# The second output projection: weights, row blocks and first splits in another order, and another place for every second row block's operands

## The chip, the cores and the metric

The kernel runs on one core of one Trainium2 chip. The metric is the time of one execution on the device in microseconds (us); three runs of a kernel are given by their median. Engine names are those of the profile: PE multiplies matrices, PEld loads its weights, DVE, ACT and POOL work elementwise, SP issues most of the transfers. A transfer is called a load when it goes from device memory (DRAM) to the chip's own memory.

## What is computed

Two layers of an encoder over 1024 rows of 1024 numbers. A layer is a token mixer, a layer norm, a gated feed-forward part and a second layer norm. The first mixer is latent attention, the second is differential attention: two softmax maps per head, subtracted. This is the end of the second mixer, where the change lies:

```python
o = jnp.einsum('bhqk,bkhe->bqhe', a.astype(v.dtype), v)   # a = p[:, 0] - lam * p[:, 1]
o = _rmsnorm(o, g_sub) * (1.0 - lambda_init)
return o.reshape(b, s, DIFF_HEADS * DIFF_V) @ w_o
...
h = _layernorm(ALPHA * h + mix, ln_mix_g[i], ln_mix_b[i])
```

All of it is float32. The kernel writes a float32 operand as a high part (cast to a shorter format) plus a low part (what the cast lost) and multiplies high by high, high by low and low by high, so that one product of 128 x 128 by 128 x 512 is three matmuls.

## The kernel before

**Stages.** Mixer A, its output projection (`out_proj`), feed-forward 0, mixer B, its output projection (class `OutProj`), feed-forward 1. Only `OutProj` and the place where it is called change.

**What surrounds the change.** Mixer B goes through 8 heads of 8 row blocks (128 rows each), the last head in the order `LAST_ORDER = (6, 7, 4, 5, 2, 3, 0, 1)`. For a row block and a head PE makes the scores (`s_b`, line 220), DVE adds the bias and takes the extreme (`mx_b`, line 223), ACT exponentiates (line 228), DVE takes reciprocals (line 1429), POOL scales one map (line 1430) and DVE subtracts it (line 1431); PE transposes the result (`pt_b`), ACT and DVE split it (`pth_b`, `ptl_b`, lines 251 and 252), and PE multiplies with the values (`o_b`, line 263) for two row blocks at once. The scores have three PSUM tiles. A table (`fill`, filled by `at`) hangs further work on the steps of this loop ("slots"); within that, a scheduler that simulates the engines sets the order in which each engine's queue is written. Each engine works through its queue in order.

**The output projection.** For each row block the output is a sum over heads of `o` times `w_o`. For the row blocks 6 and 7 (`first` and `second`) the first six heads (`HEADS = 6`) are summed in `early`, within the last head's loop, from a copy of `o` in DRAM (`of`); the last two heads follow in `late`, from the tile `bo` that is still on the chip. The other six row blocks are done whole in `rest`, which also makes the layer norm. A product is `zp_a` (line 418); `oh_a` and `ol_a` are the high and low part of `o`, made by ACT (line 406) and DVE (line 407) in `split`; `z_a` is the row block of x to which DVE adds the product (line 426).

**Where the tiles lie.** The weights of a head are a high and a low half of 0.5 MB each. Those of the heads 0 to 5 are one tile of 1 MB each (`wo`) in the projection's pool, whose space was that of the transposed x (`xT`) until the last values (`bv`) are made. Those of the heads 6 and 7 lie in a ring of three pairs of tiles (`who`, `wlo`) that also holds the operands of row block 6 and that mixer B's weights and the feed-forward part use before and after. The operands of row block 7 have a tile of the pool (tag `oh`), those of the blocks 4, 5, 2, 3, 0 and 1 a tile each of the five "big" tiles (1 MB each), which also hold the rows `z_a` of two blocks at a time and the norm's factors (`gb`, two loads issued by POOL, line 448).

**The start of a row block.** `of` issues the load of `o`, takes the tiles, issues the load of the rows x and makes the split at once, for the row blocks 6 and 7 in the constructor:

```python
for tb in LAST_ORDER[:2]:
    self.of(tb)
```

All loads named here but those of `gb` are issued by SP, into one queue.

Of the kernel before, what the change touches and what calls it, by code (L numbers as in the profile page):

```python
# [38 lines left out]
LAST_ORDER = (6, 7, 4, 5, 2, 3, 0, 1)  # L39
# [3 lines left out]
def trunk(  # L43
# [66 lines left out]
    def big_tile(name, dt=F32R):  # L110
        return big.tile([P, 2, 1024], dt, tag="big", name=name)
# [13 lines left out]
    def small(name, n=1):  # L125
        return sp.tile([P, 2], F32, tag="small", name=name, bufs=22)[:, :n]
# [159 lines left out]
    def out_proj(side, w_o, o_dram, x_src, x_dst, lng, lnb, xo):  # L286


        with tc.tile_pool(name="op0", bufs=2, side=side, reuse_waits="tile") as pool:
# [21 lines left out]
            for tb in LAST_ORDER:  # L311
                nm = f"a0_{tb}"
                of = pool.tile([P, H, P], F32, tag="of", name=f"of_{nm}", bufs=2)
                src = o_dram[tb // 2][:, :, (tb % 2) * P:(tb % 2) * P + P]
                nc.sync.dma_start(of, src.rearrange("h p q -> p h q"))
                ot = pool.tile([P, 2, D], F32R, tag="oh", name=f"oh_{nm}").rearrange("p a (h q) -> p a h q", h=H)
                oh, ol = ot[:, 0], ot[:, 1]
# [31 lines left out]
    class OutProj:  # L349
# [5 lines left out]
        def __init__(self, side, w_dr, o_dram, o_here, x_src, x_dst, scale):  # L355
            self.st = ExitStack()
            self.pool = self.st.enter_context(tc.tile_pool(name="op1", bufs=2, side=side, reuse_waits="tile"))
            self.o_dram, self.o_here, self.x_src, self.x_dst, self.scale = o_dram, o_here, x_src, x_dst, scale
            self.oh, self.z, self.sums, self.m = {}, {}, {}, {}
            for tb in LAST_ORDER[:2]:  # L360
                self.of(tb)
            self.wo = []
            for h in range(H):
                if h < self.HEADS:
                    t = self.pool.tile([P, 2, D], F32, tag=f"wo{h}", name=f"wo1_{h}", bufs=1)
                    nc.sync.dma_start(t, w_dr[h])
                    t = t.bitcast(F32R)
                    self.wo.append((t[:, 0], t[:, 1]))
                else:
                    t = [wp.tile([P, D], F32, tag=f"w{p}", name=f"w{p}o1_{h}") for p in "hl"]  # L370
                    for p in range(2):
                        nc.sync.dma_start(t[p], w_dr[h][:, p])
                    self.wo.append([x.bitcast(F32R) for x in t])

        def of(self, tb):

            nm, n = f"a1_{tb}", self.HEADS
            k = LAST_ORDER.index(tb)
            first = k < 2
            of = (wp if k < 4 else self.pool).tile(  # L380
                [P, H, P], F32, tag="wr" if k < 4 else f"z{LAST_ORDER[k % 2]}", name=f"of_{nm}", bufs=2 if k < 4 else 1,
            )[:, :n]
            src = self.o_dram[tb // 2][:n, :, (tb % 2) * P:(tb % 2) * P + P]
            nc.sync.dma_start(of, src.rearrange("h p q -> p h q"))
            if tb == LAST_ORDER[0]:
                hl = [wp.tile([P, D], F32R, tag=f"w{p}", name=f"o{p}_{nm}") for p in "hl"]
            else:
                if first:
                    t = self.pool.tile([P, 2, D], F32R, tag="oh", name=f"oh_{nm}", bufs=1)
                else:  # L390
                    t = big_tile(f"oh_{nm}")
                hl = [t[:, p] for p in range(2)]
            self.oh[tb] = [t.rearrange("p (h q) -> p h q", h=H) for t in hl]
            if first:
                self.z[tb] = self.pool.tile([P, D], F32, tag=f"z{tb}", name=f"z_{nm}", bufs=1)
            elif k % 2 == 0:
                self.pair = big_tile(f"z_{nm}", F32)
            if not first:
                self.z[tb] = self.pair[:, k % 2]
            nc.sync.dma_start(self.z[tb], self.x_src[tb * P:(tb + 1) * P, :])  # L400
            self.sums[tb] = small(f"sum_{nm}", 2)
            self.split(tb, slice(0, n), of)

        def split(self, tb, hs, o):
            oh, ol = (t[:, hs] for t in self.oh[tb])
# [655 lines left out]
    early = ast.enter_context(tc.tile_pool(name="a1e", bufs=1))  # L1061
# [130 lines left out]
    with ast as st:  # L1192
# [97 lines left out]
        def at(slot, fn, *args):  # L1290
            fill.setdefault(slot, []).append(lambda: fn(*args))
# [57 lines left out]
    with ExitStack() as st:  # L1349
# [165 lines left out]
        first, second = LAST_ORDER[:2]  # L1515
# [6 lines left out]
        b = 8 * (H - 1) - 2  # L1522
        at(b, begin_out)
        for slot, what, args in (
            (3, "early", (first, (0, 1))), (4, "early", (first, (2, 3))), (5, "early", (first, (4, 5))),
            (8, "early", (second, tuple(range(H - 2)))), (9, "late", (first,)),
        ):
            at(b + slot, lambda what, *a: getattr(proj[0], what)(*a), what, *args)
# [97 lines left out]
```

## Time and profile before

| | |
|---|---|
| median of three runs | 2262.74 us (2262.04 to 2263.79) |
| profiled execution, time | 2264.72 us |
| profiled execution, span of the core | 2263.0 us |
| mean granted clock of PE | 0.998 |
| PE busy | 2239.2 us, 99% of the span |
| PEld / DVE / ACT / POOL busy | 1912.2 / 1545.3 / 1014.7 / 776.2 us |
| matmuls | 11410 |
| chain that ended last, PE's share | 95% |
| q1, the queue that SP issues into | 277.44 MB, 34.6% of 16 engines |

The table is the page of the profiled execution, the only one of which there is a trace; its time lies 1.98 us above the median of the runs. Busy time counts from an instruction's start to its modelled end; PE's instructions overlap, so that a busy PE can still wait for operands. The part of the trace that matters here lies between 1480 and 1680 us: to about 1549 us the rest of mixer B runs together with `early` and the first `late`, from there to 1620 us `rest`, and behind it feed-forward 1.

### The profile page before, as it was taken

To read this page: it belongs to the slowest core of one execution; us is meant where nothing else is said; L and a number is where in the kernel's file an instruction comes from. 1 tells how busy PE (TensorE), PEld (TensorE's weight loads), DVE (VectorE), ACT (ScalarE), POOL (GpSimd) and SP (SyncE) were. 2 spreads that over 40 slices of the span, in tenths; PEclk is the share of its full clock that TensorE was granted. 3 is DMA by queue.
4 is the path that set the end of the run, shared out by engine and by line. 5 is a ranking of instruction groups with operands and counts; after the bars stand their busy time and mean duration, and the time that the engine had idled before them with its cause. 6 is when DMAs were issued, how large, how long until landed. Compare 5 with 4: busy or idle time off the path is not lost.

```text
span 2263.0 us, 31059 instructions
## 1 busy us (share of the span) xinstructions
PE 2239.2 (99%) x11410; PEld 1912.2 (84%) x11410; DVE 1545.3 (68%) x2894; ACT 1014.7 (45%) x2097; POOL 776.2 (34%) x626
## 2 busy tenths in 40 slices
PE   8999999999999999999999999999999999999998
PEld 8999998888888888888888898878788888888886
DVE  5676765596766667777576667576787656658778
ACT  4455664352333334444465656564432333334444
POOL 2232341114444440455432424221114444430561
PEclk9999999999999999999999999999999999999999
DMA  5010125434435338454320212063344232238443
GB/s 204 14 35 31 42 71 188 147 122 155 171 133 202 115 127 327 181 194 157 99 52 22 69 34 62 23 223 124 128 144 165 82 108 102 103 113 325 162 180 150
DMA packets 105545, 287.76 MB, mean 127 GB/s; under 512 B 7968, under 2 KB 30112, under 8 KB 94896
## 3 DMA queue, kind: packets, MB, share of 16 engines
q1 hardware_dynamic: 101552, 277.44, 34.6%
q0 software_dynamic: 3840, 8.33, 1.4%
q8 instruction: 90, 1.47, 0.3%
q14 instruction: 63, 0.52, 0.1%
HBM read 204.47 MB, written 77.07 MB: 124 GB/s over the span
## 4 chain that ended last, share of the span: by engine, by line
PE 95%; DVE 2%; DMA 1%; issue 1%; ACT 1%; POOL 0%; SPq 0%; DVEq 0%; POOLq 0%; ACTq 0%
PE gb L548 15%; PE ga L548 10%; PE gc L548 10%; PE dw L872 7%; PE dx L872 5%; PE s_a L220 4%; PE zp_a L418 3%; PE s_b L220 3%; PE dv L872 3%; PE dy L872 3%; PE bp L145 3%; PE bp L143 3%; PE bp L144 3%; PE o_a L263 2%; PE o_b L263 2%; PE hq L1123 2%
## 5 line engine op out<-in xcount | busy, mean ns | idle before, releaser
L504 ACT CAST op_g<-gr 128x512 fp32r<-128x512 f32 x240 | 146.9, 621 | 377.3 <-PE gb L548 189.9
L505 POOL TENSOR_TENSOR op_g<-gr,op_g 128x512 fp32r<-128x512 f32 x104 | 146.0, 1409 | 254.1 <-ACT op_g L504 143.9
L505 DVE TENSOR_TENSOR op_h<-rh,op_h 128x512 fp32r<-128x512 f32 x152 | 142.3, 962 | 50.0 <-ACT op_h L504 50.0
L548 PE MATMUL ga<-xh_m,op_g 128*128 128x512 f32 x512 | 168.2, 389 | 0.0
L872 PE MATMUL dw<-op_w_t,op_h 128*128 128x512 f32 x660 | 151.3, 390 | 0.0
L504 ACT CAST op_h<-rh 128x512 fp32r<-128x512 f32 x152 | 91.8, 619 | 124.6 <-PE dx L872 34.9
L872 PEld LDWEIGHTS dw<-op_w_t,op_h 128*128 128x128 f32 x660 | 123.6, 188 | 25.9 <-DVE op_h L505 0.3
L228 ACT ACTIVATE l_b<-l_b,mx_b 128x256 f32<-128x256 f32 (+7 forms) x128 | 99.4, 777 | 73.2 <-DVE mx_b L223 71.2
L505 POOL TENSOR_TENSOR op_w_b<-rw_b,op_w_b 128x512 fp32r<-128x512 f32 x44 | 64.5, 1488 | 175.1 <-ACT op_w_b L504 167.8
L505 DVE TENSOR_TENSOR op_g<-gr,op_g 128x512 fp32r<-128x512 f32 x136 | 112.0, 827 | 17.4 <-ACT op_g L504 17.2
L872 PE MATMUL dx<-op_w_b,op_h 128*128 128x512 f32 x528 | 121.5, 390 | 1.0 <-DVE op_w_b L505 1.0
L1430 POOL TENSOR_SCALAR l_b<-l_b,rb,cst 128x128 f32<-128x128 f32 (+3 forms) x64 | 52.8, 825 | 198.9 <-DVE rb L1429 187.5
L872 PEld LDWEIGHTS dx<-op_w_b,op_h 128*128 128x128 f32 x528 | 98.8, 188 | 23.0 <-DVE op_w_b L505 2.6
L548 PE MATMUL gb<-t3h_f,op_g 128*128 128x512 f32 x352 | 115.5, 389 | 1.0 <-DVE tmp L637 1.0
L548 PE MATMUL gb<-t2h_f,op_g 128*128 128x512 f32 x352 | 115.4, 390 | 0.4 <-DVE op_g L505 0.4
L548 PE MATMUL gc<-t1h_f,op_g 128*128 128x512 f32 x352 | 115.6, 389 | 0.1
L548 PE MATMUL gb<-t4h_f,op_g 128*128 128x512 f32 x352 | 115.5, 389 | 0.0
L548 PE MATMUL gc<-b22h_f,op_g 128*128 128x512 f32 x352 | 115.3, 389 | 0.0
L505 POOL TENSOR_TENSOR op_g<-s,op_g 128x512 fp32r<-128x512 f32 x40 | 56.1, 1403 | 166.4 <-ACT op_g L504 158.4
L548 PEld LDWEIGHTS ga<-xh_m,op_g 128*128 128x128 f32 x512 | 96.1, 188 | 20.0
L143 PE MATMUL bp<-xT_f,h_wb 128*128 128x512 f32 x256 | 101.8, 398 | 0.0
L144 PE MATMUL bp<-xT_f,h_wb 128*128 128x512 f32 x256 | 101.5, 397 | 0.0
(388 smaller groups left out, 6690.8 us busy)
## 6 DMA issues: line engine op xcount, KB each, us to landing
gr<-in_w_gu SPq DMA_DIRECT2D x44, 1024.0 KB, 6.8
rh<-h_dr SPq DMA_DIRECT2D x28, 1024.0 KB, 4.8
h_dr<-sh SPq DMA_DIRECT2D x22, 1024.0 KB, 5.1
h_dr<-hp SPq DMA_DIRECT2D x22, 768.0 KB, 4.1
tt<-in_w_dn SPq DMA_DIRECT2D x22, 512.0 KB, 7.5
rh<-h_dr SPq DMA_DIRECT2D x12, 768.0 KB, 4.3
wo_dr<-op_pwo SPq DMA_DIRECT2D x16, 512.0 KB, 3.4
z<-xs_dr SPq DMA_DIRECT2D x16, 512.0 KB, 12.0
```

The lines of the kernel that those rows point to most:

```text
L143: T.matmul(ps_out, lh, rh, start=(i == 0), stop=False)
L144: T.matmul(ps_out, lh, rl, start=False, stop=False)
L145: T.matmul(ps_out, ll, rh, start=False, stop=(i == n - 1))
L220: T.matmul(s[:, :w], lh, rh[:, ks], start=(j == 0), stop=(j == len(q_pass) - 1))
L228: ends["exp"] = A.activation(l[:, :n], l[:, :n], AF.Exp, bias=mx, scale=-1.0, accum_out=sm).ins
L263: T.matmul(po[:, c], a, b[:, j % 2, c], start=st, stop=sp_, skip_group_check=True)
L418: T.matmul(m, a[:, h, :], self.wo[h][w][:, c], start=(start and h == heads[0] and a is oh and w == 0), stop=(stop and h == heads[-1] and a ...
L504: turns["cast"] = A.copy(hi, src).ins
L505: return eng.tensor_tensor(lo, src, f32(hi), ALU.subtract).ins
L548: T.matmul(o, w[:, a, k * P:(k + 1) * P], x[b][:, k, :], start=(first and k == 0 and (a, b) == (0, 0)), stop=(k == 3 and a == 1), skip_gro ...
L872: T.matmul(o, h[:, a, c], w[:, b_], start=(first and (a, b_) == (0, 0)), stop=(last and a == 1), skip_group_check=True,).ins for a, b_ in ...
L1430: G.tensor_scalar(l1[:, :n], l1[:, :n], r[:, 1:2], nlam, ALU.mult, ALU.mult)
```

## The change

- The weights of the heads 0 and 1 now lie in the ring and those of the heads 2 to 7 in the pool's tiles.
- The constructor issues the loads in this order: row block 6's `o`, the weights of the heads 0 to 5, with row block 6's rows x ahead of head 6, row block 7's `o` and its rows, and the weights of the heads 6 and 7. The scheduler puts some of them elsewhere, as shown below.
- The splits of the row blocks 6 and 7 are no longer made in the constructor. They are called `first_split` and hang on the table 0 and 6 slots behind it.
- Two of the three parts of `early` for row block 6 hang one slot earlier (2 and 3 instead of 3 and 4).
- The row blocks 5, 3 and 1 have their operands in the pool's one tile `oh`, as row block 7 had; of the big tiles the blocks 4, 2 and 0 take one each.

```diff
-            for tb in LAST_ORDER[:2]:
-                self.of(tb)
+            self.of(LAST_ORDER[0])
             self.wo = []
             for h in range(H):
-                if h < self.HEADS:
+                if h == 6:
+                    self.load_z(LAST_ORDER[0])
+                if h == self.HEADS:
+                    self.of(LAST_ORDER[1])
+                    self.load_z(LAST_ORDER[1])
+                if h > 1:
                     t = self.pool.tile([P, 2, D], F32, tag=f"wo{h}", name=f"wo1_{h}", bufs=1)
...
-                if first:
+                if k % 2:
                     t = self.pool.tile([P, 2, D], F32R, tag="oh", name=f"oh_{nm}", bufs=1)
                 else:
                     t = big_tile(f"oh_{nm}")
...
+            self.sums[tb] = small(f"sum_{nm}", 2)
+            if first:
+                self.loaded[tb] = of
+            else:
+                self.load_z(tb)
+                self.split(tb, slice(0, n), of)
+
+        def load_z(self, tb):
             nc.sync.dma_start(self.z[tb], self.x_src[tb * P:(tb + 1) * P, :])
-            self.sums[tb] = small(f"sum_{nm}", 2)
-            self.split(tb, slice(0, n), of)
+
+        def first_split(self, tb):
+            self.split(tb, slice(0, self.HEADS), self.loaded.pop(tb))
...
-            (3, "early", (first, (0, 1))), (4, "early", (first, (2, 3))), (5, "early", (first, (4, 5))),
+            (0, "first_split", (first,)),
+            (2, "early", (first, (0, 1))), (3, "early", (first, (2, 3))), (5, "early", (first, (4, 5))),
+            (6, "first_split", (second,)),
             (8, "early", (second, tuple(range(H - 2)))), (9, "late", (first,)),
```

No instruction is added or removed. Up to the last head of mixer B and from feed-forward 1 on, every engine has the same instructions in the same order; between them three places matter.

**SP's queue, at the constructor, before** (the number behind a name is the head or the row block, the last one counts tiles; 128x1024 is 0.5 MB, 128x2048 is 1 MB):

```order
L372 DMA wlo_6_14976<-wo_dr_95 128x1024
L372 DMA who_6_14975<-wo_dr_95 128x1024
L384 DMA of_a_4_15581<-o_dr_2_87 128x6x128
L372 DMA wlo_7_14980<-wo_dr_96 128x1024
L400 DMA z_a_6_14950<-xs_dr_98 128x1024
L400 DMA z_a_7_14958<-xs_dr_98 128x1024
L366 DMA wo_0_14963<-wo_dr_89 128x2048
L366 DMA wo_1_14965<-wo_dr_90 128x2048
```

**The same place after:**

```order
L376 DMA who_0_14952<-wo_dr_89 128x1024
L376 DMA wlo_0_14953<-wo_dr_89 128x1024
L376 DMA wlo_1_14957<-wo_dr_90 128x1024
L376 DMA who_1_14956<-wo_dr_90 128x1024
L370 DMA wo_2_14960<-wo_dr_91 128x2048
L370 DMA wo_3_14962<-wo_dr_92 128x2048
L370 DMA wo_4_14964<-wo_dr_93 128x2048
L370 DMA wo_5_14966<-wo_dr_94 128x2048
L412 DMA z_a_6_14950<-xs_dr_98 128x1024
L412 DMA z_a_7_14972<-xs_dr_98 128x1024
L370 DMA wo_6_14975<-wo_dr_95 128x2048
L370 DMA wo_7_14977<-wo_dr_96 128x2048
```

Head 0's weights stand where head 6's stood, and ahead of head 2's stand 2 MB of loads, where ahead of head 0's there were 2.9 MB; row block 4's `o` and the rows x of blocks 6 and 7 have moved behind head 5's.

**PE's queue, the first products of the projection, before** (`zp_a_6_0` is the left half of row block 6's product, `zp_a_6_1` the right half):

```order
L263 MATMUL o_b_3_15030<-pth_b_6_3_14938,bvl_7_14865 128x128
L220 MATMUL s_b_4_0_0_15059<-bk_10192,bq_10190 128x320
L220 MATMUL s_b_4_0_0_15059<-bk_10192,ql_10195 128x320
L418 MATMUL zp_a_6_0_0_15160<-wo_0_14963,oh_a_6_14948 128x512 x2
L418 MATMUL zp_a_6_0_0_15160<-wo_0_14963,ol_a_6_14949 128x512
L418 MATMUL zp_a_6_1_0_15167<-wo_0_14963,oh_a_6_14948 128x512 x2
L418 MATMUL zp_a_6_1_0_15167<-wo_0_14963,ol_a_6_14949 128x512
L148 MATMUL pt_b_6_0_15085<-ident,l_b_6_0_14890 128x128 x4
```

**And after** (ahead of the first row shown stand the five products of head 0 that need its weights alone, and ahead of these the third of the last head's four scores of row block 6):

```order
L431 MATMUL zp_a_6_0_0_15108<-who_1_14956,oh_a_6_14948 128x512
L431 MATMUL zp_a_6_0_0_15108<-wlo_1_14957,oh_a_6_14948 128x512
L431 MATMUL zp_a_6_0_0_15108<-who_1_14956,ol_a_6_14949 128x512
L431 MATMUL zp_a_6_1_0_15115<-who_0_14952,ol_a_6_14949 128x512
L431 MATMUL zp_a_6_1_0_15115<-who_1_14956,oh_a_6_14948 128x512
L431 MATMUL zp_a_6_1_0_15115<-wlo_1_14957,oh_a_6_14948 128x512
L431 MATMUL zp_a_6_1_0_15115<-who_1_14956,ol_a_6_14949 128x512
L431 MATMUL zp_a_6_0_0_15108<-wo_2_14960,oh_a_6_14948 128x512 x2
L431 MATMUL zp_a_6_0_0_15108<-wo_2_14960,ol_a_6_14949 128x512
L431 MATMUL zp_a_6_1_0_15115<-wo_2_14960,oh_a_6_14948 128x512 x2
L431 MATMUL zp_a_6_1_0_15115<-wo_2_14960,ol_a_6_14949 128x512
L220 MATMUL s_b_6_1_1_14908<-bk_10192,bq_10190 128x448
```

Before, the first product stands behind all scores of the row blocks 6 and 7; now 18 products (heads 0 to 2) stand ahead of the fourth score of row block 6.

**PE's queue in `rest`, where row block 2 follows row block 5, before** (`xTp_a` are transposes of a finished row block):

```order
L418 MATMUL zp_a_5_1_0_15707<-who_7_14979,oh_a_5_15674 128x512
L148 MATMUL xTp_a_4_0_15746<-ident,z_a_4_15584 128x128 x4
L148 MATMUL xTp_a_4_1_15754<-ident,z_a_4_15584 128x128 x4
L418 MATMUL zp_a_2_0_0_15772<-wo_0_14963,oh_a_2_15764 128x512 x2
L418 MATMUL zp_a_2_1_0_15798<-wo_0_14963,oh_a_2_15764 128x512 x2
L418 MATMUL zp_a_2_0_0_15772<-wo_0_14963,oh_a_2_15764 128x512
```

**And after:**

```order
L431 MATMUL zp_a_5_1_0_15707<-wo_7_14977,oh_a_5_15674 128x512 x3
L431 MATMUL zp_a_2_0_0_15772<-who_0_14952,oh_a_2_15764 128x512
L431 MATMUL zp_a_2_0_0_15772<-wlo_0_14953,oh_a_2_15764 128x512
L431 MATMUL zp_a_2_0_0_15772<-who_0_14952,oh_a_2_15764 128x512
L431 MATMUL zp_a_2_0_0_15772<-who_1_14956,oh_a_2_15764 128x512
L431 MATMUL zp_a_2_0_0_15772<-wlo_1_14957,oh_a_2_15764 128x512
L431 MATMUL zp_a_2_0_0_15772<-who_1_14956,oh_a_2_15764 128x512
L431 MATMUL zp_a_2_0_0_15772<-wo_2_14960,oh_a_2_15764 128x512 x3
L431 MATMUL zp_a_2_0_0_15772<-wo_3_14962,oh_a_2_15764 128x512 x3
L148 MATMUL xTp_a_4_0_15746<-ident,z_a_4_15584 128x128 x4
```

The transposes of block 4 have moved from the boundary of two row blocks to the middle of the second one's first half, and the left half's products now stand together.

More of the change, by code (lines that the diff above doesn't have):

```diff
@@ L358, in __init__ @@
             self.o_dram, self.o_here, self.x_src, self.x_dst, self.scale = o_dram, o_here, x_src, x_dst, scale
-            self.oh, self.z, self.sums, self.m = {}, {}, {}, {}
-            for tb in LAST_ORDER[:2]:
-                self.of(tb)
+            self.oh, self.z, self.sums, self.m, self.loaded = {}, {}, {}, {}, {}
+            self.of(LAST_ORDER[0])
             self.wo = []
             for h in range(H):
-                if h < self.HEADS:
+                if h == 6:
[4 more added lines that the diff above has]
+                if h > 1:
                     t = self.pool.tile([P, 2, D], F32, tag=f"wo{h}", name=f"wo1_{h}", bufs=1)
```

## The prediction

> **What bounds the kernel now.** I read the page first, then the chain of waits in order of time, the timelines of PE and SP around the first products, the queues in short windows, and PE's waits in `rest`.
>
> ```profile
> span 2263.0 us, 31059 instructions
> PE 2239.2 (99%) x11410; PEld 1912.2 (84%) x11410; DVE 1545.3 (68%) x2894; ACT 1014.7 (45%) x2097; POOL 776.2 (34%) x626
> PE 95%; DVE 2%; DMA 1%; issue 1%; ACT 1%; POOL 0%; SPq 0%; DVEq 0%; POOLq 0%; ACTq 0%
> ```
>
> PE is the bound, with 95% of the chain that ended last, and the change leaves its 11410 matmuls as they are. So only waits of PE can be won or added. The chain's rows around the change say where they are (start, length, what):
>
> ```profile
> 1491.61 12.13 DMA wo<-wo_dr
> 1543.89 5.53 PE zp_a L418 x24
> 1560.46 9.33 PE zp_a L418 x41
> ```
>
> One matmul of a product costs 9.33 / 41 = 0.2276 us. The load of head 0's weights is on the chain, 12.13 us long, because PE waits for it. The first six of the 24 matmuls from 1543.89 are the last of `late`: mixer B's end lies at 1543.89 + 6 x 0.2276 = 1545.3. There I measure what the early part of the change does; the late part I measure in `rest`.
>
> **Early part: the loads.** PE at the first products (start, length, then the instruction and in brackets the idle time before it):
>
> ```profile
> 1493.14 0.36 PE L220 MATMUL s_b<-bk,bq 128*128 128x448 f32 x1
> 1493.34 0.37 PE L220 MATMUL s_b<-bk,ql 128*128 128x448 f32 x1
> 1493.96 0.47 PE L220 MATMUL s_b<-bk,bq 128*128 128x448 f32 x1 [0.25 <-DVE mx_b L223]
> 1495.23 0.50 PE L220 MATMUL s_b<-bk,bq 128*128 128x512 f32 x1 [0.59 <-DVE mx_b L223]
> 1496.52 1.06 PE L148 MATMUL pt_b<-ident,l_b 128*128 128x128 f32 x8 [0.55 <-DVE l_b L1431]
> 1500.03 0.50 PE L220 MATMUL s_b<-bk,bq 128*128 128x512 f32 x1 [0.15 <-DVE mx_b L223]
> 1503.79 0.73 PE L418 MATMUL zp_a<-wo,oh_a 128*128 128x512 f32 x2 [0.74 <-DMA wo<-wo_dr]
> 1509.42 0.63 PE L148 MATMUL pt_b<-ident,l_b 128*128 128x128 f32 x4 [0.25 <-DVE l_b L1431]
> ```
>
> The score at 1493.96 is the one that stands behind 18 products after the change. Before it PE idled little while it had scores: the six bracketed waits from 1493.96 on sum to 0.25 + 0.59 + 0.55 + 0.15 + 0.74 + 0.25 = 2.5 us. Now SP's issues, and the same loads from issue to landing (KB each, median us; one load in each row):
>
> ```profile
> 1487.61 0.33 SPq L372 DMA_DIRECT2D wlo<-wo_dr  x1
> 1487.99 0.42 SPq L372 DMA_DIRECT2D who<-wo_dr  x1
> 1491.61 5.18 SPq L366 DMA_DIRECT2D wo<-wo_dr  x6
> ```
>
> ```profile
> who<-wo_dr SPq DMA_DIRECT2D x1, 512.0 KB, 5.0
> wo<-wo_dr SPq DMA_DIRECT2D x1, 1024.0 KB, 12.1
> ```
>
> And the queues' packets, MB and share of the 16 engines in four windows of 2 us, from 1494 (second queue only), 1496, 1500 (second queue only) and 1502 (first only):
>
> ```profile
> q0 software_dynamic: 37, 0.15, 18.4%
> ...
> q1 hardware_dynamic: 112, 0.42, 51.0%
> q0 software_dynamic: 111, 0.41, 50.5%
> ...
> q0 software_dynamic: 30, 0.06, 7.9%
> ...
> q1 hardware_dynamic: 119, 0.84, 99.9%
> ```
>
> SP's queue (q1) moves 0.84 / 2 = 0.42 MB/us alone, and 0.21 while POOL's two `gb` loads (q0) run, from about 1495 to 1500.5. POOL's issues keep their place.
>
> Head 0's halves take the places of 1487.61 and 1487.99, so they land at 1487.99 + 5.0 = 1493.0. PE is done with the third score at 1493.34 + 0.20 = 1493.54 and has no wait there; five products on head 0 take 5 x 0.2276 = 1.14, to 1494.7. Head 1's halves are 1.05 MB behind them: 0.84 MB until 1495, 0.21 MB at half rate, landed at 1496.0, a wait of 1.3 us. Seven products take it to 1497.6. Head 2 is again 1.05 MB: 0.95 until 1500.5 at half rate, the rest at 0.42, landed at 1500.75. The same sum for before (3.0 MB behind 1493.0, landed by this at 1502.9) comes 0.8 us short of the 1491.61 + 12.13 = 1503.74 of the trace, so I take the middle, 1501.2: a wait of 3.6 us. Six products take 1.4, and the score stands at 1502.55 instead of 1493.96, **8.6 us later**.
>
> A rule of the Trainium skill bears on this, page "DMA: Bandwidth & Descriptors", section "Queues, rings and completion order": each DMA engine takes packets in turn from the rows of queues that have work for it. The trace agrees (51.0% and 50.5% of the engines for q1 and q0 from 1496 to 1498). It speaks against the change, as the loads that it wants soonest fall into the shared stretch; without sharing head 2 would land at 1493.0 + 2.1 / 0.42 = 1498.0 and the score start at 1499.4, 3.2 us sooner.
>
> **Early part: what is made good.** While PE waits, DVE, ACT and POOL have no new scores, and the chain of the softmax starts 8.6 us later. From the fourth score to the end of `late` it was 1545.3 - 1493.96 = 51.3 us. In that stretch 18 products (4.1 us) are no longer to be done, and PE's small waits may go: the 2.5 us above, and with each a refilling of the pipe, which I put at 0.1 us (from 0.37 - 0.2276, a lone matmul's length over its share), 0.6 for six. So 51.3 - 4.1 - 3.1 = 44.1 us is the least. The most is 51.3, when the chain of softmax steps and not PE's work sets the pace. Between them decides how full DVE is (length, then busy us of PE, PEld, DVE, ACT, POOL):
>
> ```profile
> 1500.00:1540.00 40.00, 38.99 (x226) 33.43 (x227) 31.14 (x87) 25.95 (x64) 10.14 (x12) 1.00 0.60 239
> ```
>
> DVE is busy 31.14 / 40 = 78%; squeezed into 45.65 / 51.3 of the time it would be 87%, which a queue of short instructions can still do. I take half of the 3.1 us as left, 45.65: the nearest row, PE's 38.99 of 40 us, says that PE's own work sets the pace. End: 1502.55 + 45.65 = 1548.2 against 1545.3, **+2.9 us**. Bounds: -2.0 if PE finds every weight there (rival 1), +8.6 if the chain keeps its 51.3.
>
> **Late part.** Before, the five big tiles make a row block's operands wait for a tile that the block before last, or its rows, still holds; the pool's tile for every second block lets a split begin one block earlier. PE's transposes of each finished block (five of them, behind two rows that price them):
>
> ```profile
> 1553.10 1.03 PE L148 MATMUL xTp_a<-ident,z_a 128*128 128x128 f32 x8
> 1553.89 0.48 PE L418 MATMUL zp_a<-wo,oh_a 128*128 128x512 f32 x1
> ...
> 1569.62 1.03 PE L148 MATMUL xTp_a<-ident,z_a 128*128 128x128 f32 x8
> 1581.98 1.03 PE L148 MATMUL xTp_a<-ident,z_a 128*128 128x128 f32 x8
> 1594.38 1.03 PE L148 MATMUL xTp_a<-ident,z_a 128*128 128x128 f32 x8
> 1607.24 1.03 PE L148 MATMUL xTp_a<-ident,z_a 128*128 128x128 f32 x8
> 1620.11 1.03 PE L148 MATMUL xTp_a<-ident,z_a 128*128 128x128 f32 x8
> ```
>
> and whom PE waited for from 1569 to 1611 (total, times, longest):
>
> ```profile
> PE zp_a L418 <- ACT oh_a L406: 0.7, 4, 0.2
> PE zp_a L418 <- DVE oh_a L407: 0.6, 2, 0.3
> ```
>
> Four blocks took 1620.11 - 1569.62 = 50.49 us. Work: 48 matmuls (8 heads, two halves, three each) x 0.2276 = 10.92, and eight transposes 1553.89 - 1553.10 = 0.79, so 4 x 11.71 = 46.86. Lost: 3.6 us, a third of it named waits for splits, the rest small stops around them. With splits one block ahead I take **-3.3**; bounds 0 (the order of DVE and ACT, not the tile, makes them late) and -3.6. The transposes move into the next block's first half, where the norm that feeds them has some 3 us more.
>
> **At nothing.** The rows x and heads 6 and 7 move behind head 5 in SP's queue, and row block 4's `o` behind those: by 0.42 MB/us from 1501.2, four loads of heads (4.2 MB) end at 1511, rows x at 1514, heads 6 and 7 at 1519, all after 1503.79 and ahead of `late`, which ends at 1545.3; PE needs the rows only through DVE's addition, heads 6 and 7 only in `late`. If this cover fails, each costs the queue's lag, 0.52 / 0.42 = 1.2 us for a half-MB load. Block 7's split hangs at slot 6, its products at slot 8 as before. The tightest cover is that of feed-forward 1's first weights (`gp`): block 2's rows x now stand ahead of them in SP's queue, and their tile is free only when DVE has split block 4. The split, the issue, the cast that needs the first load, and PE in feed-forward 1:
>
> ```profile
> 1533.43 1.95 DVE L407 SCALAR_TENSOR_TENSOR oh_a<-of_a,cst,oh_a 128x768 fp32r<-128x768 f32 x2
> ...
> 1534.48 10.30 SPq L564 DMA_DIRECT2D gp<-in_w_gu  x3
> ...
> 1541.18 0.62 ACT L504 CAST op_gp<-gp 128x512 fp32r<-128x512 f32 x1 [0.89 <-PE zp_a L418]
> ...
> 1630.25 21.77 PE ga L548 x96
> ```
>
> 2.9 us later the split ends at 1538.3; the load, some 4.1 us without a queue (row of line 400 below), lands at 1542.4, the cast would come at 1544.1: 1.7 us to spare. Without them ACT holds block 5's split by what is missing. Ring tiles that feed-forward 1 finds free earlier win nothing, as PE is full there (21.77 / 96 = 0.2268 us a matmul).
>
> **Sum.** +2.9 - 3.3 = -0.4 us against the profiled execution (2264.7, 2.0 above the median), so 2264.3 there and **2262.3** against the median of 2262.74.
>
> **The rivals.**
> 1. *Faster: the loads are there when PE asks.* For it: a half-MB load of line 400 took as little as 3.1 us (row below), so 1 MB without a queue 3.1 + 0.52 / 0.42 = 4.4 us, and head 2, issued at about 1491.6, would land at 1496.0. Against it: 12.1 us for the 1 MB load that was queued, and q0's share. Then PE does the 18 products without a wait, the score starts at 1493.54 + 4.1 = 1497.6, `late` ends at 1543.3, -2.0; with -3.3 it is -5.3: 2257.4 us.
>
> ```profile
> DMA to landing us min/median/max: 3.1/4.1/10.3
> ```
>
> The same page, section "Anatomy of one DMA", has a fixed part near 2 us plus bytes over 436 GB/s, an estimate of 4.4 us for 1 MB by itself; no run here shows such a load alone.
>
> 2. *Slower: the softmax chain keeps its pace.* The fourth score of block 6 starts 8.6 us later, and the chain of its followers, of which DVE's 78% and waits such as `mx_b` are part, needs the same 51.3 us; PE then idles at the end of mixer B for what it did early. +8.6 - 3.3 = +5.3: 2268.0 us. It is slower by over 0.2% if more than 7.8 us of the 8.6 come out at the end. For it: four of the six waits above are for DVE. Against it: they are 0.15 to 0.59 us long, and PE has products to put in between.
>
> 3. *The late gain does not come.* Splits stay late as DVE does the norm of the block before ahead of them; for it: DVE is a releaser in those rows with 0.3 us at most. +2.9: 2265.6 us.
>
> **How the numbers follow.** Chances: my forecast 0.60 (its own range 2259.5 to 2264.8, from a landing of head 2 between 1500.75 and 1501.6, 44.1 to 46.5 us, and -2.5 to -3.6 late), rival 1 0.18, rival 2 0.10, rival 3 0.12. About 0.2%, 4.5 us, can be told from no change: faster is below 2258.2, slower above 2267.3. Rival 1 and 0.02 of the forecast's edge are faster, 0.20; rival 2 and 0.01 slower, 0.11; the rest 0.69 the same. The range takes in rival 1 with half its spread, and rival 3 with 1 us above, 2256.8 to 2266.6, and leaves out rival 2 and half of rival 1, 0.19.
>
> **What would show it.** In the profile after: PE waiting 1.3 us for `who` or `wlo` and 3.6 us for `wo` between 1494 and 1502; the score behind them near 1502.5; the end of `late` near 1548; transposes `xTp_a` 11.8 us apart instead of 12.4 to 12.9, with no waits for `oh_a`. I am wrong if those load waits are missing (rival 1), if PE idles for `l_b` or `pth_b` from 1530 on (rival 2), or if the transposes stay 12.4 us apart (rival 3).

## The result, and the profile after

The changed kernel takes 2258.57 us (median of 12 runs, 2257.11 to 2260.77) against 2263.82 for the one before (12 runs; the three runs ahead of the prediction had 2262.74), ratio 0.9978 with a 95% interval of 0.9970 to 0.9986: 5 us or 0.22% faster. A second timing beside other kernels gave 2258.44 and 0.9978 (0.9968 to 0.9987). The predicted 2262.3 is 3.7 us too high, and as a change the prediction had -0.4 us where -5.3 were measured. The time lies within the range of 2256.8 to 2266.6, but below the forecast's own part of it, which went no lower than 2259.5: it lies where the range was widened for rival 1, near that rival's price, and was not reached by rival 1's way.

The page of after, as that of before in the prediction (span, then busy time by engine):

```profile
span 2257.6 us, 31061 instructions
PE 2236.1 (99%) x11410; PEld 1912.8 (85%) x11410; DVE 1543.2 (68%) x2894; ACT 1013.5 (45%) x2097; POOL 773.6 (34%) x626
```

PE is still the bound. Its busy time fell by 3.1 us with the same 11410 matmuls, so it contains stops too; what was won is therefore read below from the starts of equal matmuls. PE's timeline where the first products stand, and the first product of row block 4, with which mixer B's end is reached:

```profile
1493.37 0.36 PE L220 MATMUL s_b<-bk,ql 128*128 128x448 f32 x1
1493.57 0.39 PE L431 MATMUL zp_a<-who,oh_a 128*128 128x512 f32 x1
...
1497.81 0.74 PE L431 MATMUL zp_a<-wo,oh_a 128*128 128x512 f32 x2 [1.18 <-DMA wo<-wo_dr]
...
1499.32 0.37 PE L220 MATMUL s_b<-bk,bq 128*128 128x448 f32 x1
...
1512.29 0.63 PE L148 MATMUL pt_b<-ident,l_b 128*128 128x128 f32 x4 [0.30 <-DVE l_b L1444]
...
1544.90 0.40 PE L431 MATMUL zp_a<-who,oh_a 128*128 128x512 f32 x1
```

PE does the products of the heads 0 and 1 without a wait, waits once, 1.18 us for head 2, and has the fourth score at 1499.32; I had put 1.3 and 3.6 us and 1502.55. Mixer B ends at 1544.90. Before, the first product of row block 4 is this one:

```profile
1545.16 4.25 PE L418 MATMUL zp_a<-wo,oh_a 128*128 128x512 f32 x18
```

So the early part ends 0.3 us earlier, not 2.9 later. (Counted from the third score, mixer B ends after 51.53 us here and after 51.13 and 51.33 us in two more profiles of after, against 51.82 and 51.83 in two of before: 0.3 to 0.7 us.) In `rest`, the transposes of after, and the first matmul of feed-forward 1:

```profile
1572.16 1.03 PE L148 MATMUL xTp_a<-ident,z_a 128*128 128x128 f32 x8
1581.21 1.03 PE L148 MATMUL xTp_a<-ident,z_a 128*128 128x128 f32 x8
1593.89 1.03 PE L148 MATMUL xTp_a<-ident,z_a 128*128 128x128 f32 x8
1604.76 1.03 PE L148 MATMUL xTp_a<-ident,z_a 128*128 128x128 f32 x8
1616.53 1.03 PE L148 MATMUL xTp_a<-ident,z_a 128*128 128x128 f32 x8
...
1617.32 0.48 PE L561 MATMUL ga<-xh_m,op_gp 128*128 128x512 f32 x1
```

The distance is no longer even (9.1 to 12.7 us), since the transposes now stand inside the next row block. From the first to the last of these it is 1616.53 - 1572.16 = 44.4 us where before took 50.5, but 180 products stand between them instead of 192. With the 12 others (12 x 0.2276 = 2.7 us) it would be 47.1: 3.4 us less than before, and 0.2 us above the 46.86 us of pure work. No wait for `oh_a` is left. Why they were late before is seen at row block 2 (ACT's split and PE's first product of it, before):

```profile
1569.82 0.94 ACT L406 ACTIVATE oh_a<-of_a,cst 128x768 fp32r<-128x768 f32 x1 [6.30 <-PE zp_a L418]
1570.81 0.50 PE L418 MATMUL zp_a<-wo,oh_a 128*128 128x512 f32 x1 [0.15 <-ACT oh_a L406]
```

and after:

```profile
1560.54 0.94 ACT L419 ACTIVATE oh_a<-of_a,cst 128x768 fp32r<-128x768 f32 x1 [2.65 <-PE zp_a L431]
1569.43 0.39 PE L431 MATMUL zp_a<-who,oh_a 128*128 128x512 f32 x1
```

Before, the split could start only behind the last product of row block 5 (it ends at 1569.38 + 0.39 = 1569.77), 1.0 us ahead of its use, and PE waited for it; after, it starts 8.9 us ahead of its use. The places of the tiles in the built kernels say why: before, the operands of the blocks 5, 2, 3, 0 and 1 all lie in one and the same of the five big tiles, so that each split waits for the products of the block right ahead; after, the pool's tile and big tiles take turns.

Feed-forward 1 begins at 1617.32, before at:

```profile
1620.90 0.48 PE L548 MATMUL ga<-xh_m,op_gp 128*128 128x512 f32 x1
```

From mixer B's end to there it is 72.42 us instead of 75.74: 3.3 us less. What is left of the 5.4 us between the spans lies behind: from that matmul to the end 640.3 instead of 642.1 us. In the first 80 us of feed-forward 1 PE had one wait before, and none after:

```profile
PE gb L548 <- DVE tmp L637: 1.0, 1, 1.0
```

### The profile page after: what moved, and what is told of

The parts are those of the page before. It is cut to its first block, busy times and chain, and to the rows that moved or that the text cites. A ratio compares the mean times of both kernels' runs of the same rounds, so it can differ in the third digit from the quotient of the medians.

```text
span 2257.6 us, 31061 instructions
## 1 busy us (share of the span) xinstructions
PE 2236.1 (99%) x11410; PEld 1912.8 (85%) x11410; DVE 1543.2 (68%) x2894; ACT 1013.5 (45%) x2097; POOL 773.6 (34%) x626
## 4 chain that ended last, share of the span: by engine, by line
PE 96%; DVE 1%; ACT 1%; DMA 1%; issue 0%; POOL 0%; SPq 0%; DVEq 0%; POOLq 0%
PE gb L561 16%; PE gc L561 10%; PE ga L561 10%; PE dw L885 8%; PE dx L885 5%; PE zp_a L431 4%; PE s_a L220 4%; PE s_b L220 3%; PE dv L885 3%; PE dy L885 3%; PE bp L145 3%; PE bp L143 3%; PE bp L144 3%; PE o_a L263 2%; PE o_b L263 2%; PE hq L1136 2%
## 5 line engine op out<-in xcount | busy, mean ns | idle before, releaser
L518 POOL TENSOR_TENSOR op_w_b<-rw_b,op_w_b 128x512 fp32r<-128x512 f32 x44 | 64.4, 1486 | 172.6 <-ACT op_w_b L517 172.6
```

Of the source, the lines that this page charges most:

```text
L518: return eng.tensor_tensor(lo, src, f32(hi), ALU.subtract).ins
```

## The experiments

For all kernels two pieces of a profile are compared, which hold 622 and 2783 matmuls in each kernel: from the row block 6's third score (start of its second matmul) to the first matmul of feed-forward 1 (piece 1), and from there to the end (piece 2). What lies ahead of the third score is the same program, but it differed by up to 3 us from profile to profile (1490.80 to 1493.89).

| kernel | median us | ratio (95%) | piece 1 | piece 2 |
|---|---|---|---|---|
| before, two profiles | 2263.2 to 2263.8 | 1 | 127.56, 127.55 | 642.1, 641.5 |
| after, three profiles | 2258.57, 2258.44 | 0.9978 | 123.95, 123.55, 123.74 | 640.3, 640.5, 640.3 |
| late part alone | 2260.48 | 0.9988 (0.9980 to 0.9997) | 125.67 | 640.8 |
| early part alone | 2266.31 | 1.0012 (1.0003 to 1.0021) | 128.07 | 643.3 |
| split in front | 2260.97 | 0.9988 (0.9979 to 0.9997) | 125.40 | 640.8 |
| half loads | 2258.41 | 0.9978 (0.9970 to 0.9987) | 123.63 | 640.4 |
| late part, cast behind | 2262.08 | 0.9994 (0.9985 to 1.0002) | 123.75 | 643.7 |
| `gb` by SP | 2256.65 | 0.9971 (0.9960 to 0.9982) | 122.72 | 640.4 |
| late part, both behind | 2260.69 | 0.9988 (0.9979 to 0.9997) | 124.08 | 642.2 |
| early part, transposes behind | 2265.01 | 1.0007 (0.9998 to 1.0016) | 128.52 | 642.2 |
| `gb` last | 2262.74 | 0.9995 (0.9987 to 1.0004) | 124.37 | 643.5 |

**The late part alone.** The kernel before with

```diff
-                if first:
+                if k % 2:
                     t = self.pool.tile([P, 2, D], F32R, tag="oh", name=f"oh_{nm}", bufs=1)
```

> The kernel before, with one edit: the operands of the row blocks 5, 3 and 1 lie in the pool's tile, as after. Theory (the terms add, and `rest` is one of them): mixer B's end stays at 1545.2 us, the transposes of finished row blocks come 11.7 us apart instead of 12.4 to 12.9, feed-forward 1's first matmul comes 3.3 us earlier than before, and the time falls by 3.3 to 3.6 us (2260.3, ratio 0.9985). Rival (the gain of `rest` needs the early part too, as the earlier loads of row blocks leave ACT and DVE free): the distance stays above 12.2 us and the time falls by less than 1.5 us. On feed-forward 1, where after gained another 1.3 us: if the ring tiles that heads 6 and 7 no longer hold make it, nothing of it shows here; if it is the landing time of one store (4.9 us before, 3.8 after) that differs from run to run, it may show here too.

The time came as the theory had it (2260.48), the way did not: `rest` gained its 3.3 us (72.39 from mixer B's end to feed-forward 1), piece 2 another 0.7 to 1.3 without any ring tile being moved, and 1.5 us were lost ahead of `rest`. The gain in `rest` is the firmest number of all: that stretch takes 72.39 to 72.42 us in eight profiles with the pool's tile (three of after, this one, half loads, `gb` by SP, and the late part with the cast and with both behind), against 75.74 and 75.72 in the two of before. Where the 1.5 us were lost, ACT's timeline shows, and PE's behind it:

```profile
1541.21 1.14 ACT L504 CAST op_gp<-gp 128x512 fp32r<-128x512 f32 x2 [2.49 <-DMA gp<-in_w_gu]
1542.26 0.36 ACT L251 CAST pth_b<-pt_b 128x256 fp32r<-128x256 f32 x1
```

```profile
1542.67 0.38 PE L263 MATMUL o_b<-pth_b,bvh 128*128 128x256 f32 x1 [0.95 <-ACT pth_b L251]
```

The cast of `gp` stands where it stood before, but its load now lands later, behind block 2's rows; `pth_b` is queued behind the cast and PE waits for it. It is the cover that the prediction called the tightest, and alone the pool's tile breaks it. In after the scheduler had put the cast behind `pth_b` and the norm's squares (it runs at 1543.67, without a wait).

**The early part alone.** After, with the edit above taken back.

> The kernel after, with one edit undone: the operands of the row blocks 5, 3 and 1 lie in the big tiles, as before. Theory (the terms add): mixer B's end at 1544.9 as after, 0.3 us earlier than before; `rest` as long as before (transposes 12.4 to 12.9 us apart); feed-forward 1 0 to 1.3 us shorter; time down by 0.3 to 1.6 us (ratio 0.9993 to 0.9999), the same within what can be told. Rival (the early part carries more than its term, since it also frees ACT and DVE at the start of `rest`): down by 3 us or more.

Neither: it is slower than before, by 2.6 us in the medians. Piece 1 is 0.5 us longer than before, piece 2 longer by 1.2 to 1.9. The waits of PE in feed-forward 1 name two places:

```profile
PE gb L561 <- DVE tmp L650: 1.4, 1, 1.4
PE xTp_a L148 <- DVE z_a L184: 1.1, 1, 1.1
```

The scheduler put the transposes of the last row block behind 24 products of feed-forward 1, where before and after have them behind 36; DVE has not finished the norm there. So the two parts of the change do not add: alone they give -3.3 and +2.6, together -5.3.

**The first split back in the constructor.**

```diff
             self.of(LAST_ORDER[0])
+            self.first_split(LAST_ORDER[0])
...
-            (0, "first_split", (first,)),
```

> The kernel after, with row block 6's first split made in the constructor again, ahead of the weights' loads. Theory (the split's place decides which ring tile it gets, and so when head 0's weights can be loaded): SP issues head 0's first load at about 1487.6 instead of 1484.7, head 2's weights land about 3 us later than after, and mixer B ends 1 to 3 us later (time 2259.5 to 2261.5). Rival (PE has scores enough to fill the time, so the landing does not matter): the loads are 3 us later, but mixer B ends within 0.5 us of after, time 2258.6. Second rival (the loads' start is not set by the tile): issues as after.

The theory holds for the loads: SP issues head 0 at 1485.52 here, 5.73 us ahead of the third score as in before; in after it is 8.67 us (1484.70). Head 1, ahead of whose loads row block 4's `o` stands here as in before, is then late:

```profile
1497.14 0.50 PE L432 MATMUL zp_a<-who,oh_a 128*128 128x512 f32 x1 [1.19 <-DMA who<-wo_dr]
```

Piece 1 is 1.65 us longer than after's, the time 2.4 us. That this is all due to the landing is not shown: with the split the scheduler also moved 12 of the 18 products behind scores, and a wait of 2.0 us for DVE (`nmu_a`) appeared.

**Loads of 4 KB a partition.**

```diff
-                    nc.sync.dma_start(t, w_dr[h])
+                    if h in (2, 3):
+                        for p in range(2):
+                            nc.sync.dma_start(t[:, p], w_dr[h][:, p])
+                    else:
+                        nc.sync.dma_start(t, w_dr[h])
```

> The kernel after, with the weights of the heads 2 and 3 loaded in two halves of 0.5 MB each (4 KB a partition) instead of 1 MB (8 KB a partition). Theory (two queues share the engines packet by packet, so that a queue with packets twice as long gets twice the bytes): from 1496 to 1500 us SP's queue and that of `gb` move equal bytes, near 0.42 MB each in 2 us, instead of 0.58 and 0.28; head 2's weights land about 1 us later than after's 1497.8, PE's wait for them grows from 1.2 to some 2.2 us, and the time grows by 0 to 1 us. Rival (each queue's share is set by something else, such as the number of its loads under way): 0.58 against 0.28 MB again, and head 2 lands at 1497.8.

The queues (packets, MB, share of the engines), after from 1496 to 1498:

```profile
q1 hardware_dynamic: 77, 0.58, 68.7%
q0 software_dynamic: 73, 0.29, 35.8%
```

and this kernel from 1494 to 1496:

```profile
q0 software_dynamic: 112, 0.41, 51.8%
q1 hardware_dynamic: 110, 0.40, 49.8%
```

The packets are shared evenly in both; the bytes follow the packets' size. That part of the theory is shown. The landing moved little: PE's wait for head 2 ends 4.68 us behind the third score instead of 4.44 (4.12 and 4.28 in after's other profiles), 0.2 to 0.6 us later and not the 1 us of the theory, and the time is after's. Why it is no more is open.

**The late part, with the cast of `gp` behind the squares.** The late part alone, and in the places that make these instructions (`...` marks what is left out):

```diff
+        if name == "a1_6":
+            ends["squares6"] = squares[1].ins
...
+                if layer == 1 and n == 0:
+                    behind(turns["cast"], ends["squares6"])
```

> The kernel with the pool's tile alone (blocks 5, 3 and 1), in which ACT's first casts of feed-forward 1's weights `gp` now stand behind the squares of row block 6's norm. There ACT stood 2.49 us at the cast of `gp`, waiting for its load, with the split `pth_b` behind it, and PE idled 0.95 us for that. Theory (this stall is what the early part of the change takes away, and most of what it is worth beside the pool's tile): the wait for `gp` and PE's for `pth_b` go, the end of mixer B comes 1.0 to 1.5 us earlier, and the time is 2259.0 to 2259.5, within 1 us of after. Rival (the early part gains by its earlier loads and products): the stall goes, PE waits elsewhere, and the time stays at 2260.5, 2 us above after.

Half of the theory is shown: the stall is gone and piece 1 is 123.75 us, after's mean (123.75 too), with no load and no split of the early part moved. But piece 2 grew by 2.8 us, more than was won: the transposes of the last row block stand behind 24 products, and PE waits 1.4 us for them and 1.6 us at `gb`.

**The same, with those transposes held behind the 36th product.** (The expectation says 27th for where they had stood; the count is 24.) Here `i` is a transpose and `done_a` the matmuls of one product of feed-forward 1:

```diff
+                if name == "a1_1":
+                    behind(i, ends["gate"])
...
+                if (n, pr) == (0, "2"):
+                    ends["gate"] = done_a[-1]
```

> The kernel of the run before it (the pool's tile alone, casts of `gp` behind the squares), with the transposes of the last row block held in PE's queue behind the 36th product of feed-forward 1, where after has them; in the run before they stood behind the 27th and PE waited 1.4 us for the last norm there. Theory (the pool's tile is the whole gain, and the early part of the change is worth nothing by itself beside good orders of ACT's and PE's queues): those waits go, feed-forward 1 takes 640.3 to 641 us to the end, the time is 2258.3 to 2259.3, within 0.7 us of after without one load moved. Rival (feed-forward 1 is late for another reason, the ring's tiles): it takes over 642 us again and the time stays above 2261.

A miss. Piece 1 stays (124.08), the two waits go, but two others come, and piece 2 is 642.2:

```profile
PE ga L552 <- ACT pg L625: 0.8, 1, 0.8
PE gb L552 <- ACT op_g L508: 0.6, 1, 0.6
```

Holding one instruction moved others in ACT's and DVE's queues. So a version without the early part that is as fast as after was not found, although its piece 1 is as short.

**The early part alone, with those transposes held in the same way.**

> The early part alone (odd row blocks in the big tiles), with the transposes of the last row block held behind the 36th product of feed-forward 1 in the same way. Theory: its loss against before (2.6 us) was for the most part PE's 1.1 us at those transposes and 1.4 us behind them in feed-forward 1; they go, and the time is 2263.0 to 2264.3, the same as before within 0.7 us. Rival (the early part itself costs this, by loads that come later for `rest` and feed-forward 1): the time stays at 2265.5 or more.

Between the two: 2265.01. Piece 2 is 1.1 us shorter than in the early part alone, and piece 1 is 1.0 us longer than before's; PE waits there, ahead of mixer B's end, 0.7 us for `oh_a` (ACT) and 0.5 us for `ol_a` (DVE). What the early part costs by itself beyond the queues' order is not separated by this.

**`gb` by SP, and `gb` last.** In the first, `nc.gpsimd.dma_start(gb[:, i], ...)` of `rest` becomes `nc.sync.dma_start`; in the second it is also put behind head 7's load.

> The kernel after, with the two loads of `gb` issued by SP instead of POOL: one of them (0.5 MB) then stands ahead of head 2's weights in SP's queue, the other behind head 7's, and head 2's 6 products stand behind the fourth score. No second queue is left. Theory (sharing cost head 2 about 0.9 us, the half MB ahead costs 1.25): head 2 lands 0 to 0.6 us later than after, head 3 and later sooner, SP's queue moves 0.84 MB in every 2 us; PE does two row blocks' scores meanwhile, and its wait for weights of 1.2 us falls below 0.5; the end of mixer B 0 to 1 us earlier, time 2257.6 to 2258.6. Rival (what PE does not wait for here it waits for at the softmax): the time stays at 2258.5.

> The kernel after, with the two loads of `gb` issued by SP behind head 7's weights, so that neither a second queue nor half a MB stands beside or ahead of head 2's; PE's queue begins as after's, with 18 products ahead of the fourth score. Theory (the queue of `gb` slows head 2's load): SP's queue moves 0.84 MB in every 2 us, PE's wait for head 2 falls from 1.0 to 1.2 us to 0.1 to 0.4, and the fourth score starts 0.8 to 1.0 us sooner after the third one than in after (5.95 us). Of this 0 to 0.9 us come out at the end of mixer B; time 0 to 1 us below after's of the same call. Rival (head 2's load is bound by its start or its own length): the wait stays above 0.8 us.

The first did a little better than expected: the wait for weights fell to 0.3 us and piece 1 to 122.72.

```profile
PE zp_a L431 <- DMA wo<-wo_dr: 0.3, 1, 0.3
```

At 0.9971 (0.9960 to 0.9982) it may be the fastest of all, but its interval overlaps after's. In the second, SP's queue has the engines to itself (0.83 to 0.86 MB in each 2 us from 1492 to 1500), PE waits 0.57 us for head 2, between theory and rival, and the fourth score starts 5.33 us behind the third, 0.3 to 0.6 us sooner than in after (5.95, 5.61 and 5.77 in three profiles). The time is a miss: the scheduler had made other queues again, with the transposes behind 24 products and the same two waits of 1.1 and 1.4 us, and piece 2 is 643.5.

**Before and after, again.**

> The kernel before, for a second profile. In the first one PE waited 0.97 us in feed-forward 1, behind a load `gr` that SP issued only when a store `pg_dr` had landed, 4.9 us after its issue; in the profiles of after and of three others the store took 3.8 to 4.2 us. If the store's time differs by chance, it is near 4 us here, the wait is gone or small, and from the first matmul of feed-forward 1 to the end it is 641 us or less instead of 642.1; if it belongs to the kernel before, 4.9 and 642.1 us again.

> The kernel after, for a second profile. If the pieces of the first one are this kernel's, the third score of row block 6 to the first matmul of feed-forward 1 takes 123.95 us again (within 0.3), and from there to the end 640.3 us (within 0.5); a larger difference says how far one profile carries.

> The kernel after, timed beside the run above on the same chip: 2258.0 to 2259.0 us, ratio 0.9978.

In before's second profile the store took 3.9 us, the wait fell from 0.97 to 0.64 us and piece 2 from 642.1 to 641.5. It looks as if the store's time made the difference, but the starts of equal matmuls say otherwise. The one behind that wait, in the first profile and then in the second:

```profile
1674.76 0.47 PE L548 MATMUL gb<-t3h_f,op_g 128*128 128x512 f32 x1 [0.97 <-DVE tmp L637]
```

```profile
1675.29 0.47 PE L548 MATMUL gb<-t3h_f,op_g 128*128 128x512 f32 x1 [0.64 <-DVE tmp L637]
```

It starts 53.86 and 53.85 us behind the first matmul of feed-forward 1; in all three profiles of after it is 52.67. So 1.2 us are lost in both profiles of before, with the long store and with the short one, and at the 2300th matmul the lag is 1.3 us in both. In the second one the wait is shorter because PE had lost 0.3 us earlier. DVE, for which PE waits, is late by two steps, in the first profile and then in the second:

```profile
1668.49 0.69 DVE L585 TENSOR_TENSOR gr<-gr 128x512 f32<-128x512 f32 x1 [1.25 <-DMA gr<-in_w_gu]
...
1672.82 1.19 DVE L585 TENSOR_TENSOR gr<-gr 128x512 f32<-128x512 f32 x1
```

```profile
1668.46 0.69 DVE L585 TENSOR_TENSOR gr<-gr 128x512 f32<-128x512 f32 x1 [0.36 <-DMA gr<-in_w_gu]
...
1672.80 1.74 DVE L585 TENSOR_TENSOR gr<-gr 128x512 f32<-128x512 f32 x1
```

The first waits for the load `gr`; the second is long, 1.19 and 1.74 us, and ends 0.55 us behind the end of an operation of POOL (`op_g`) in both. In after DVE does not wait for `gr`, the second operation starts 0.25 us ahead of POOL's and takes 0.68 us. So it fits that DVE, once late, is held by POOL, but no run tests this, and two profiles do not say whether every execution of before has the lag. The other 0.5 us between before's two profiles arise behind the 2300th matmul, over 500 us later, where after's three differ by 0.2 us as well. After's pieces agree within 0.4 us over three profiles, so the bound of 0.3 that was set was a little tight; the time came as expected.

## Why the prediction was right or wrong

- **PE is the bound, and only waits can move:** right, PE's 11410 matmuls and 99% stay.
- **The late part, -3.3:** right. 75.74 to 72.42 us, and the late part alone shows the same without the early one. Rival 3 is out. That transposes would come 11.8 us apart was wrong; their sum with equal products was right (47.1 us against 4 x 11.8 = 47.2). Which tile is waited for was not: it is held by the block right ahead, not by "the block before last, or its rows".
- **The stretch from the fourth score to mixer B's end, 45.65 us:** right. 1544.90 - 1499.32 = 45.58, and 45.52 and 45.56 in after's other profiles. That it fits to 0.1 us is luck, as "half of the 3.1" was a choice between 44.1 and 51.3. The softmax chain did not keep its 51.3 us (rival 2 is out).
- **Where that stretch begins, 1502.55:** wrong by 3.2 us, and this is the step that made +2.9 of what was -0.3. It had two errors that made the landing of head 2 too late (1501.2 instead of 1497.8), and a third that hid a part of them.

  First, "head 0's halves take the places of 1487.61 and 1487.99". SP's waits from 1475 to 1492, before and then after, show that it is not the place in SP's queue but the tile that decides:

```profile
SPq L372 <- PE bv L145: 12.5, 2, 11.1
```

```profile
SPq L376 <- PE bp L145: 8.3, 1, 8.3
```

  The ring's tile that is free first (when PE is done with `bp`) went to block 6's operands before, as the split stood in the constructor (ACT makes it at 1484.72); the weights got the next one, held until the last `bv`. With the split in its slot (ACT: 1490.71) the weights get the first. The places of the tiles in the built kernels say the same: before and with the split in front, block 6's operands have the tile of `bp`'s last weights, in after head 0's weights have it. The prediction has no term for the split's move; it was worth 2.9 us of SP's issue, as the run with the split in front shows.

  Second, half rate by bytes. The row that I used (112 and 111 packets, 0.42 and 0.41 MB) is from a stretch where SP's loads had 4 KB a partition. The page of the Trainium skill, "DMA: Bandwidth & Descriptors", section "Queues, rings and completion order", has the taking of turns by packets; the trace agrees (77 and 73 packets), and head 2's longer packets moved 0.29 MB/us instead of 0.21. I had read packets and reckoned in bytes.

  The third error goes the other way. With the loads 2.9 us sooner the prediction's own 0.42 MB/us would have landed head 1 at 1492.6; it landed at 1494.7 (issued at 1488.06, behind a wait of 2.2 us for `bv`, and 6.6 us long). Already alone, SP's queue moved less than the 0.84 MB in 2 us that were reckoned with; four windows of 2 us from 1486 on, after:

```profile
q1 hardware_dynamic: 142, 0.55, 90.9%
q1 hardware_dynamic: 215, 0.78, 106.6%
q1 hardware_dynamic: 148, 0.54, 81.3%
q1 hardware_dynamic: 127, 0.73, 103.7%
```

  Why it was slower is open. Of the 3.4 us at head 2, 1.3 are there at head 1 (1494.7 against 1496.0), and 2.1 come between the two, where the queue was shared. That the landing came so near the 1498.0 that the prediction gives for no sharing at all is chance: the loads did share.
- **At nothing:** but for the split's move these covers held in after; PE waits for no rows x and for no weights behind head 2's, and the cast of `gp` does not wait. Ahead of the rows x there are three loads of heads left (3 to 5), not the four of the prediction's sum; nothing hung on it.
- **Feed-forward 1, nothing to win:** wrong by 1.3 us, which both profiles of before lose against all three of after within the first 240 matmuls; some 0.5 us more differ from execution to execution. That freed ring tiles did it is out, since the late part alone moves no ring tile and reaches that matmul after 52.73 us as well. The store's time alone does not explain it, as shown above. What makes DVE earlier in after is open.
- **The gain of rival 1:** its time (2257.4) was near, its mechanism was half there: the wait for the loads is 1.0 to 1.2 us, not 0, and mixer B ends 0.3 to 0.7 us earlier, not 2.0.
- **The terms add:** this was assumed without a word, and is wrong. The tile alone breaks the cover of `gp` (125.67 against 123.75 us in piece 1, 1.9 us, which the early part happens to mend by where the scheduler puts the cast), and the early part alone costs 2.6 us.

What the early loads themselves are worth: in piece 1 next to nothing beside a good place of the cast (123.55 to 123.95 us with them, 123.75 and 124.08 without), probably as PE has scores to do meanwhile. What is shown of the 5.3 us is the 3.3 of the pool's tile in `rest`; the rest is 0.3 to 0.7 us ahead of it and 1.3 us in feed-forward 1, whose causes are open.

## What to carry to other kernels

When an instruction that takes a tile of a ring is moved, ask which tile each of the others gets now: here a split moved by 6 us let a load start 2.9 us sooner, though the load's place in its queue was the same. Cost a queue that shares engines by its packets and their size. And where a scheduler writes the queues, judge a part by the piece of the profile that it touches: a change elsewhere in the order moved feed-forward 1 by up to 3 us, as much as the part itself was worth, and two parts measured alone (-3.3 and +2.6) did not add up to the whole (-5.3).

## What the runs showed of the hardware

Two queues share the 16 engines packet by packet: 110 and 112 packets gave 0.40 and 0.41 MB with packets of one size, 77 and 73 gave 0.58 and 0.29 MB with packets twice as long in one of them. A store of 1 MB took 4.9 us in one execution and 3.9 in another of the same kernel, at the same place. A queue that is alone does not always reach one rate: SP's loads moved 0.54 to 0.78 MB in 2 us from 1486 to 1494 in after, and 0.83 to 0.86 from 1492 to 1500 in the run with `gb` last.
